# Banded attention: where the reciprocal row sums are transposed, and when the work that closes a head pair is issued

## The chip, the cores and the metric

The kernel runs on one core of one Trainium2 chip. The metric is device time in microseconds (us) of one execution, the median over several runs. A profiled execution also leaves a trace: start, length and releaser of each instruction on each engine.

The engines: PE (TensorE) multiplies matrices and transposes, and writes only to PSUM, a small memory of banks of 128 x 512 floats. DVE (VectorE) and ACT (ScalarE) read PSUM; POOL (GpSimd) works here on the main on-chip memory (SBUF) alone. SP (SyncE) issues all DMAs of this kernel, in order. "PEld" is the load of a matmul's fixed operand; it lies beside the matmul before it.

## The reference, cut to what matters

The model is one inference step of a two-layer encoder. Layer 0 mixes latent attention (A) and a banded attention (B), layer 1 is a windowed attention (C). The change is in B:

```python
B_HEADS, B_HEAD_DIM, CHUNK, B_PAST_CHUNKS, SEQ = 8, 64, 64, 8, 2048

def _grouped_attend(q, k, v, valid, scale, bias=None, sinks=None):
    s = jnp.einsum('...qhgd,...khd->...hgqk', q, k).astype(jnp.float32) * scale
    if bias is not None:
        s = s + bias.astype(jnp.float32)
    s = jnp.where(valid, s, NEG_INF)
    ...
        p = jax.nn.softmax(s, axis=-1)
    return jnp.einsum('...hgqk,...khd->...qhgd', p.astype(v.dtype), v)

# in _ab_layer
    mixed = jnp.concatenate([o_a * jax.nn.silu(g_a), o_b * jax.nn.silu(g_b)], axis=-1)
    return h + _rms(mixed @ w_out, post_g), state
```

Each chunk of 64 queries sees its own chunk and the 8 before it. For the 2048 prompt tokens the kernel works in blocks of 128 queries, each with at most five blocks of 128 keys; 64 sample tokens see 512 cached keys and their own 64.

## The kernel before

The program has five phases: input projections, attention A, attention B together with the output projection of layer 0, input projections of layer 1, attention C with its output projection. Phase 3 is the one that changes. In the trace it lies between about 1323 and 1790 us, with a tail of output projections to about 1842 us.

**Units and steps.** `GROUPS` cuts the 16 query blocks into five groups: blocks 4 to 7, 8 to 11, 12 to 15, then 2 and 3, then 0 and 1. For each group and each of the 8 heads there is one `Unit` for each block: 128 units, and 8 `Sample` units among those of the first group. A loop of 136 calls of `step(n)` runs them as a pipeline. Steps 4 to 135 stand in a `manual_schedule` for PE, DVE, ACT and SP: each of these engines runs its instructions in the order in which the Python code emits them. An engine that waits holds up all that was emitted for it later.

A step emits in this order: the exponentials of unit n+1 (ACT, L1186); the scores of unit n+2 (PE, L1176), their bias and maximum (DVE, L1180); with the first unit of a load, the Q, K and V loads of a later one (SP, L204, L1112, L1147). Then twice: some matmuls of the output projection (`J.pump`, L964) and one `turn`. A `turn` takes one of the two PSUM banks of `ps_t`, lets PE transpose one to three 128 x 128 blocks of probabilities into it (L1203), and ACT copies them to `PT` (L211, the helper `copy`). Its return value, called later in the step as one of the `lows`, lets DVE compute the low part (L214, the helper `lo_of`); with that the bank is free. Between come the products with the values (`av`, PE, L1216) into the single bank of `ps_o`, and, when a head is complete, `out`, which lets ACT copy one half (`tbm`) and DVE add the other into `OT` (L1226).

**Finish.** When both heads of a pair are complete, `out` adds a generator `finish` to the queue `J.side`; there are 24 in all, 20 of the prompt and 4 of the sample. It computes reciprocals of the row sums (DVE, L1237), loads the gate `G` (SP, L1239), spreads the reciprocals over 64 columns a head (ACT, `rb`), transposes this with PE (L1246, one block for each query block) into a bank of `ps_t` of its own, multiplies `OT` by it (DVE, L1247), multiplies by the gate (POOL, L1248) and stores (SP, L1252). `OT` has two buffers and so has the row sum `rsum`: a pair writes the ones that the pair two before it has left. A `yield` ends what one pump of the queue issues; the queue runs its first generator to the end before the next one starts. In the step the pump stands between the first `J.pump` and the first `turn`: one pump, and one more ahead of it if two or more generators are queued (L1414 to L1417).

The last `finish` of a group (`last`) queues the loads of the output projection's token tiles (`token_tile`), which `J.load.pump(1)` at the end of each step drives. After the units, `J.dense` is set and a loop runs the remaining projections.

Of the kernel before, what the change touches and what calls it, by code (L numbers as in the profile page):

```python
# [7 lines left out]
F32 = mybir.dt.float32  # L8
# [8 lines left out]
SEQ, DS, PAST, DM = 2048, 64, 1024, 1024  # L17
# [19 lines left out]
LK, YR3 = 1, 3  # L37
# [73 lines left out]
def kernel(ctx, tc, a, o, upto=5):  # L111

    nc = tc.nc
# [36 lines left out]
    ident = const.tile([128, 128], F32, name="ident")  # L150
# [59 lines left out]
    def copy(out, in_):  # L210
        nc.scalar.activation(out, in_, AF.Copy)  # L211

    def lo_of(out, x, hi, scale=1.0):
        nc.vector.scalar_tensor_tensor(out, x, scale, hi, op0=ALU.mult, op1=ALU.subtract)  # L214
# [822 lines left out]
    def jobs(banks):  # L1037
        J = K()
        J.loaded, J.ready, J.made, J.done, J.banks, J.n, J.credit = False, [], 0, 0, banks, 0, 0.0
        J.last, J.put, J.dense = False, dma, False  # L1040
        J.early, J.half, J.n_early, J.MM = [], {}, 0, {}
        J.side, J.tails, J.load, J.samp = Fill(), Fill(), Fill(), Fill()

        def bank():
            p, n = J.banks[J.n % len(J.banks)]
            J.n += 1
            return p.tile([128, 512], F32, name=n)

        def pump(rate):
            J.credit = min(J.credit + rate, rate + 1)  # L1050
            while J.credit > 0 and next(J.proj):
                J.credit -= 1

        def rest():
            J.load.pump(1)
            (J.side if J.side.q else J.samp).pump(1)
            J.tails.each()
        J.bank, J.pump, J.rest = bank, pump, rest
        return J
# [28 lines left out]
    def phase3():  # L1088
        with ExitStack() as st, ExitStack() as st_a:
# [37 lines left out]
            ps_s, ps_t = pool_a("ps_s3", 2, space=PSUM), pool("ps_t3", 2, space=PSUM)  # L1127
            ps_o, ps_p = pool("ps_o3", 1, space=PSUM), pool("ps_p3", 1, space=PSUM)
            J = jobs([(ps_p, "proj")])
# [4 lines left out]
            for i in range(NPT):  # L1134
                PT = ppt.tile([128, 2, 6, 256], F32R, name=f"PT{i}")
# [5 lines left out]
            def load_values(quad, h0, nh):  # L1141
                start, cnt = GROUPS[quad]
                b0 = max(0, start - 4)
                nb = start + cnt - b0
                V = hv.tile([128, 8, 128], F32R, name="V")[:, :nh * nb].rearrange("p (h b) x -> p h b x", h=nh)
                for h in range(nh):
                    dma(f(V[:, h]), sVB[h0 + h, b0 * 128:(b0 + nb) * 128].rearrange("(b p) x -> p b x", p=128))  # L1147
                    heads[quad, h0 + h].V = V[:, h]

            class Unit:  # L1150
# [42 lines left out]
                def turn(self, g):  # L1193
                    b0, nb = g
                    e = self.i % 2
                    if e == 0 and b0 == 0:
                        self.H.PT = PTs[turn[0] % NPT]
                        turn[0] += 1
                    PT = self.PT = self.H.PT
                    s0 = self.lo - self.base + self.off + b0  # L1200
                    t = ps_t.tile([128, 4, 128], F32, name="t")
                    for b in range(nb):
                        nc.tensor.transpose(t[:, b], self.P[:, (b0 + b) * 128:(b0 + b) * 128 + 128], ident)  # L1203
                    hi = PT[:, 0, s0:s0 + nb, e * 128:e * 128 + 128]
                    copy(hi, t[:, :nb])
                    return lambda: lo_of(PT[:, 1, s0:s0 + nb, e * 128:e * 128 + 128], t[:, :nb], hi)

                def av(self, half):

# [21 lines left out]
            def finish(hp, OT, rs, b0, nb, last=False):  # L1231

                t0 = b0 * 128
                n = min(nb * 128, T - t0)
                b0 = b0 if b0 < 16 else 0
                ri = sc.tile([128, 4, 2], F32, name="ri", bufs=2)
                nc.vector.reciprocal(ri[:, :nb], rs[:, b0:b0 + nb])  # L1237
                G = ot.tile([128, 512], F32, name="G")
                dma(G[:, :n], sG[512 + hp * 128:640 + hp * 128, t0:t0 + n])  # L1239
                rb = sc.tile([128, 4, 2, 64], F32, name="rb", bufs=1)  # L1240
                copy(rb[:, :nb], ri[:, :nb, :, None].to_broadcast([128, nb, 2, 64]))
                for _ in range(YR3 if t0 < 512 or t0 == SEQ else 2):
                    yield
                p = ps_t.tile([128, 512], F32, name="t")
                for b in range(nb):
                    nc.tensor.transpose(p[:, b * 128:b * 128 + 128], rb[:, b].rearrange("p a b -> p (a b)"), ident)  # L1246
                nc.vector.tensor_mul(OT[:, :n], OT[:, :n], p[:, :n])  # L1247
                nc.gpsimd.tensor_tensor(OT[:, :n], OT[:, :n], G[:, :n], op=ALU.mult)  # L1248
                yield
                yield  # L1250
                yield
                dma(sMB[hp * 128:hp * 128 + 128, t0:t0 + n], OT[:, :n])  # L1252
                if last:
                    for d in range(0, n, 128):
                        J.load.add(token_tile(t0 + d, min(128, n - d)))

            def token_tile(t0, r):
                ks = slice(4 if t0 in J.MM else 0, KT)
                M = ld.tile([128, DM], F32, name="M", bufs=1).rearrange("p (k t) -> p k t", k=KT)
                if t0 not in J.MM:  # L1260
                    dma(M[:, 0:4, :r], sM[:, t0:t0 + r].rearrange("(k p) t -> p k t", p=128))
                dma(M[:, 4:8, :r], sMB[:, t0:t0 + r].rearrange("(k p) t -> p k t", p=128))
                for _ in range(2 if J.dense else 4):
                    yield
                while t0 not in J.MM and J.made - J.done >= 2:
                    yield
                J.made += t0 not in J.MM
                MM = J.MM.pop(t0, None) or ld.tile([128, 2, KT, 128], F32R, name="MM", bufs=2)
                copy(MM[:, 0, ks, :r], M[:, ks, :r])
                nc.gpsimd.tensor_tensor(MM[:, 1, ks, :r], M[:, ks, :r], MM[:, 0, ks, :r], op=ALU.subtract)  # L1270
                for _ in range(DRDY3):
                    yield
                J.ready.append((MM, t0, r))
# [95 lines left out]
            def unit(n):  # L1369
                quad, h, j = units[n]  # L1370
                us[n] = Unit(quad, h, j) if j >= 0 else Sample(h)
                us[n].score()
                i = at0.get(units[n], len(loads)) + 1
                if 1 < i < len(loads):
                    load_heads(*loads[i])
                if i < 4:
                    load_bias(i)
                ahead(n + LC)
                keys(n + LK)

            load_values(*loads[0])
            W, us = [], {}
            for n in range(LC):
                ahead(n)
            for n in range(LK):
# [13 lines left out]
            def step(n):  # L1399
                cur = us.pop(n)  # L1400
                if n + 1 in us:
                    us[n + 1].exp()
                if n + 2 < len(units):
                    unit(n + 2)
                quad, h, j = units[n]
                i = at2.get(units[n], len(loads)) + 1
                if 1 < i < len(loads):
                    load_values(*loads[i])
                lows, gs = [], cur.groups()
                rate = RATEA if J.n_early else RATE3 if GROUPS[quad][1] == 4 else RATES  # L1410
                J.samp.pump(1)
                for q in range(2):
                    J.pump(rate / 3)
                    if q == 0:  # L1414
                        if len(J.side.q) > 1:
                            J.side.pump(1)
                        (J.side if J.side.q else J.samp).pump(1)  # L1417
                    if q < len(gs):
                        lows.append(cur.turn(gs[q]))
                if avs:  # L1420
                    v, half = avs.pop(0)
                    v.av(half)
                    if half and v.j == GROUPS[v.quad][1] - 1:
                        late.append(v.out)
                J.pump(rate / 3)
                for fn in lows:
                    fn()
                if cur.j < 0:
                    cur.av(1)
                    late.append(cur.out)  # L1430
                while late:
                    late.pop(0)()
                if cur.j in (1, 3):
                    avs.extend([(cur, 0), (cur, 1)])
                if not J.loaded:
                    J.load.pump(WLOAD)
                J.load.pump(1)
                J.tails.each()

            for n in range(NAUTO3):  # L1440
                step(n)
# [591 lines left out]
```

## Time and profile before

| what | value |
|---|---|
| median of 3 runs | 2735.03 us |
| the 3 runs | 2735.82, 2735.03, 2724.87 us |
| profiled execution, its own time | 2728.87 us |
| its span, first to last instruction | 2727.1 us |
| mean granted TensorE clock | 0.988 |
| DVE, ACT, POOL busy over the span | 1568.7, 1392.4, 522.1 us |

The profiled execution lies 6.2 us below the median and 4.0 us above the fastest run. The four times together have a mean of 2731.15 us. In the views, a wait is the idle time of an engine ahead of an instruction, with the instruction of another engine that ended it; "<-" points to that releaser. In the view of stretches the columns are: the stretch and its length, then busy us and number of instructions of PE, PEld, DVE, ACT and POOL, the granted clock as a share of full speed, the DMA engines' busy share and GB/s.

### The profile page before, as it was taken

What the parts mean: (1) busy time and instruction counts of PE and PEld (TensorE: products, weight loads), DVE (VectorE), ACT (ScalarE), POOL (GpSimd) and SP (SyncE); (2) the same over time, 40 slices, a digit from 0 to 9 for tenths busy, and PEclk for the clock granted to TensorE, in tenths of its full rate; (3) what the DMA queues carried; (4) which work ended last, traced back from release to release, by engine and by line L of the source; (5) the groups of instructions that cost most, each with busy time, mean ns of one, the idle gap of its engine ahead of it and who ended that gap; (6) DMA issues with size and microseconds to landing.
All of it is one profiled execution on the core that took longest, in us unless ns stands there. A gap on an engine that the chain in (4) does not pass through costs nothing. (4 is left out here: it accounts for less than half of the span.)

```text
span 2727.1 us, 46654 instructions
## 1 busy us (share of the span) xinstructions
PE 2566.5 (94%) x16296; PEld 2337.6 (86%) x16296; DVE 1568.7 (58%) x4255; ACT 1392.4 (51%) x3548; POOL 522.1 (19%) x1110
## 2 busy tenths in 40 slices
PE   7999999999999999999888999799999999999997
PEld 6999999899988888888777887679999998787886
DVE  5453345352237778787667766466223214787886
ACT  4332232422337777777666665452233223877783
POOL 0001000001002323211101333342001000344443
PEclk9999999999999999999999999999999998999999
DMA  7546444727447666651666766466425428455552
GB/s 239 171 147 209 133 143 129 255 96 234 143 118 200 194 170 188 167 155 48 194 187 167 204 191 172 149 216 224 149 96 169 127 72 246 109 139 133 137 132 70
DMA packets 382282, 437.92 MB, mean 161 GB/s; under 512 B 49936, under 2 KB 308888, under 8 KB 378816
## 3 DMA queue, kind: packets, MB, share of 16 engines
q1 hardware_dynamic: 382048, 434.95, 54.2%
q8 instruction: 129, 2.11, 0.3%
q14 instruction: 105, 0.86, 0.1%
HBM read 282.80 MB, written 157.09 MB: 161 GB/s over the span
## 5 line engine op out<-in xcount | busy, mean ns | idle before, releaser
L237 PE MATMUL pm<-X,W 128*128 128x384 f32 (+2 forms) x4536 | 752.8, 324 | 2.5 <-DVE ev L214 1.7
L237 PEld LDWEIGHTS pm<-X,W 128*128 128x128 f32 x4536 | 730.4, 189 | 6.2 <-DVE ev L214 2.3
L211 ACT ACTIVATE PT<-t 128x512 fp32r<-128x512 f32 (+3 forms) x704 | 344.5, 504 | 268.9 <-PE t L1203 113.6
L214 DVE SCALAR_TENSOR_TENSOR PT<-t,PT 128x512 fp32r<-128x512 f32 (+3 forms) x688 | 376.0, 569 | 100.8 <-ACT PT L211 99.3
L964 PE MATMUL proj<-Wo,MM 128*128 128x512 f32 (+1 forms) x1416 | 391.6, 407 | 11.3 <-ACT z L211 8.1
L964 PEld LDWEIGHTS proj<-Wo,MM 128*128 128x128 f32 (+1 forms) x1416 | 246.1, 187 | 59.5 <-ACT z L211 11.6
L214 DVE SCALAR_TENSOR_TENSOR ev<-pm,ev 128x256 fp32r<-128x256 f32 (+3 forms) x197 | 98.6, 502 | 336.9 <-ACT ev L430 102.2
L237 PE MATMUL pm<-W,X 128*128 128x256 f32 (+5 forms) x2040 | 281.2, 297 | 0.0
L237 PEld LDWEIGHTS pm<-W,X 128*128 128x128 f32 (+1 forms) x2040 | 272.0, 187 | 1.0
L702 ACT ACTIVATE P<-s,m 128x512 f32<-128x512 f32 (+9 forms) x344 | 209.3, 616 | 33.3 <-DVE m L691 30.7
L683 PE MATMUL s<-KA,Q 128*128 128x512 f32 (+7 forms) x640 | 201.1, 396 | 10.5 <-ACT P L702 8.4
L228 DVE TENSOR_TENSOR W<-R,W 128x768 fp32r<-128x768 f32 (+3 forms) x114 | 116.0, 1055 | 134.0 <-ACT W L227 133.7
L726 PE MATMUL t<-ident,P 128*128 128x128 f32 x1088 | 176.3, 276 | 3.4 <-ACT P L702 1.0
L689 DVE TENSOR_REDUCE m<-s 128x1 f32<-128x480 f32 (+7 forms) x216 | 132.4, 613 | 80.3 <-PE s L683 79.9
L726 PEld LDWEIGHTS t<-ident,P 128*128 128x128 f32 x1088 | 134.6, 141 | 41.7 <-ACT P L702 15.1
L754 PE MATMUL acc<-PT,V 128*128 128x256 f32 x1152 | 156.3, 285 | 6.6 <-DVE OT L763 6.6
L754 PEld LDWEIGHTS acc<-PT,V 128*128 128x128 f32 x1152 | 140.6, 188 | 12.0 <-PE t L726 6.0
L1702 ACT ACTIVATE P<-s,m 128x256 f32<-128x256 f32 (+2 forms) x264 | 119.4, 465 | 11.6 <-DVE m L1694 10.3
L1216 PE MATMUL acc<-PT,V 128*128 128x256 f32 x672 | 111.6, 298 | 13.7 <-DVE OT L1226 11.0
L1180 DVE CUSTOM_DVE_ANT_0 s<-s,bias 128x640 f32<-128x640 f32 (+4 forms) x128 | 95.4, 745 | 42.9 <-PE s L1176 40.7
L1693 DVE CUSTOM_DVE_ANT_0 s<-s,mask 128x256 f32<-128x256 f32 (+1 forms) x256 | 107.6, 422 | 20.2 <-PE t L1711 10.9
L683 PE MATMUL s<-KR,Q 128*128 128x384 f32 (+6 forms) x320 | 116.2, 363 | 0.6 <-DMA Q<-sQR 0.6
(248 smaller groups left out, 3927.7 us busy)
## 6 DMA issues: line engine op xcount, KB each, us to landing
Q<-sQA SPq DMA_DIRECT2D x128, 128.0 KB, 3.3
sWO<-W SPq DMA_DIRECT2D x32, 512.0 KB, 3.8
Q<-sQB SPq DMA_DIRECT2D x128, 128.0 KB, 3.1
Wo<-sWO SPq DMA_DIRECT2D x16, 1024.0 KB, 8.8
Q<-sQC SPq DMA_DIRECT2D x32, 512.0 KB, 7.7
R<-in_ab_w_in_dram SPq DMA_DIRECT2D x40, 384.0 KB, 4.1
K<-sKB SPq DMA_DIRECT2D x56, 256.0 KB, 5.6
V<-sVB SPq DMA_DIRECT2D x24, 512.0 KB, 6.7
```

Of the source, the lines that this page charges most:

```text
L211: nc.scalar.activation(out, in_, AF.Copy)
L214: nc.vector.scalar_tensor_tensor(out, x, scale, hi, op0=ALU.mult, op1=ALU.subtract)
L228: nc.vector.tensor_tensor(Wv[:, 1, k0:k1], Rv, Wv[:, 0, k0:k1], op=ALU.subtract)
L237: nc.tensor.matmul(ps, lhs(x, k), rhs(y, k), start=(j == 0), stop=(j == n - 1))
L683: nc.tensor.matmul(s[:r, :n], self.Q[:, x, self.qo:self.qo + r], rhs, start=(x == 0), stop=(x == 2))
L689: nc.vector.tensor_reduce(m[:r, j:j + 1], s[:r, :n], axis=AX.X, op=ALU.max)
L702: nc.scalar.activation(self.P[:r, o0:o0 + n], self.s.pop(j)[:r, :n], AF.Exp, bias=self.m[:r, 6:7], accum_out=acc)
L726: nc.tensor.transpose(t[:, b], self.P[:, (b0 + b) * 128:(b0 + b + 1) * 128], ident)
L754: nc.tensor.matmul(acc[:, (i // 2) % 2], H.V[:, b0 + b], PT[:, x, b], start=(b0 + b == 0 and x == 0), stop=(b0 + b == i and x == 1))
L964: nc.tensor.matmul(p, M[:, x, k, :r], W[k][:, y, cs], start=(k == k0 and t == 0), stop=(k == k1 - 1 and t == 2))
L1216: nc.tensor.matmul(acc, self.H.V[:, self.base - self.H.b0 + b], self.PT[:, x, off + b], start=(b == 0 and x == 0), stop=(b == nblk - 1 and ...
L1702: nc.scalar.activation(self.P[:, c, :w], self.s[:, c, :w], AF.Exp, bias=m[:, 1, c:c + 1], accum_out=m[:, 0, c:c + 1])
```

## The change

`finish` no longer takes a bank. It puts its transposes, one for each query block, into a list `spreads`. Each `turn` (none has more than three blocks of its own) takes one of them and transposes it into the last quarter of its own bank; after the low part DVE multiplies that 128 columns of `OT`. The reciprocal and the ACT copy that reads it now come in different pumps. What is still listed when the units have ended is transposed in a bank as before. In `step` the pump of `J.side` moves from between the first projection matmuls and the first `turn` to the end of the step: `J.rest()` holds one pump each of `J.load` and of `J.side` (or, if this is empty, `J.samp`) and a round of `J.tails`; with two or more generators queued, two pumps come ahead of it. Between the gate's multiplication and the store lie two yields, not three.

```diff
                     for b in range(nb):
                         nc.tensor.transpose(t[:, b], self.P[:, (b0 + b) * 128:(b0 + b) * 128 + 128], ident)
+
+                    while spreads and not spreads[0]:
+                        spreads.pop(0)
+                    out = None
+                    if spreads and nb < 4:
+                        x, out = spreads[0].pop(0)
+                        nc.tensor.transpose(t[:, 3], x, ident)
                     hi = PT[:, 0, s0:s0 + nb, e * 128:e * 128 + 128]
                     copy(hi, t[:, :nb])
-                    return lambda: lo_of(PT[:, 1, s0:s0 + nb, e * 128:e * 128 + 128], t[:, :nb], hi)
+
+                    def low():
+                        lo_of(PT[:, 1, s0:s0 + nb, e * 128:e * 128 + 128], t[:, :nb], hi)
+                        if out is not None:
+                            nc.vector.tensor_mul(out, out, t[:, 3, :out.shape[-1]])
+                    return low
...
                 dma(G[:, :n], sG[512 + hp * 128:640 + hp * 128, t0:t0 + n])
+                yield
                 rb = sc.tile([128, 4, 2, 64], F32, name="rb", bufs=1)
                 copy(rb[:, :nb], ri[:, :nb, :, None].to_broadcast([128, nb, 2, 64]))
-                for _ in range(YR3 if t0 < 512 or t0 == SEQ else 2):
+                yield
+                todo = [(rb[:, b].rearrange("p a b -> p (a b)"), OT[:, b * 128:min(n, b * 128 + 128)]) for b in range(nb)]
+                spreads.append(todo)
+                while todo and not J.dense:
                     yield
-                p = ps_t.tile([128, 512], F32, name="t")
-                for b in range(nb):
-                    nc.tensor.transpose(p[:, b * 128:b * 128 + 128], rb[:, b].rearrange("p a b -> p (a b)"), ident)
-                nc.vector.tensor_mul(OT[:, :n], OT[:, :n], p[:, :n])
+                if todo:
+                    p = ps_t.tile([128, 4, 128], F32, name="t")
+                    for b, (x, _) in enumerate(todo):
+                        nc.tensor.transpose(p[:, b], x, ident)
+                    for b, (_, y) in enumerate(todo):
+                        nc.vector.tensor_mul(y, y, p[:, b, :y.shape[-1]])
+                    todo.clear()
                 nc.gpsimd.tensor_tensor(OT[:, :n], OT[:, :n], G[:, :n], op=ALU.mult)
-                yield
                 yield
                 yield
                 dma(sMB[hp * 128:hp * 128 + 128, t0:t0 + n], OT[:, :n])
...
-            W, us = [], {}
+            W, us, spreads = [], {}, []
...
                     J.pump(rate / 3)
-                    if q == 0:
-                        if len(J.side.q) > 1:
-                            J.side.pump(1)
-                        (J.side if J.side.q else J.samp).pump(1)
                     if q < len(gs):
                         lows.append(cur.turn(gs[q]))
...
-                J.load.pump(1)
-                J.tails.each()
+                if len(J.side.q) > 1:
+                    J.side.pump(2)
+                J.rest()
```

## Prediction

> **What bounds the kernel now.** I read the page's busy times, the view of stretches over phase 3, PE's waits there, and the timeline around each wait.
>
> ```profile
> PE 2566.5 (94%) x16296; PEld 2337.6 (86%) x16296; DVE 1568.7 (58%) x4255; ACT 1392.4 (51%) x3548; POOL 522.1 (19%) x1110
> 1345.00:1456.00 111.00, 94.74 (x653) 76.77 (x652) 70.43 (x190) 68.66 (x178) 7.28 (x12) 0.98 0.70 196
> 1456.00:1550.00 94.00, 85.44 (x576) 74.84 (x576) 71.13 (x183) 63.06 (x152) 23.08 (x45) 1.00 0.75 197
> 1700.00:1790.00 90.00, 71.52 (x359) 57.56 (x358) 38.66 (x137) 42.01 (x122) 38.89 (x74) 0.94 0.51 155
> ```
>
> PE is busy 94% of the span. Its work doesn't change (68 transposes of `rb` before and after), so the change is worth what it takes from PE's idle time in phase 3: 16.3 and 8.6 us in the stretches of the first two groups, 18.5 us in that of the two short groups. No other engine is near its limit there; DVE comes nearest, with 71 of 94 us. PE's waits in the stretch from 1345 to 1778 us (total us, times, longest):
>
> ```profile
> PE proj L964 <- ACT z L211: 8.1, 6, 2.3
> PE t L1203 <- DVE OT L1247: 7.5, 11, 1.5
> PE t L1203 <- DVE PT L214: 7.4, 10, 1.8
> PE t L1246 <- DVE PT L214: 3.8, 3, 1.8
> PE t L1203 <- DVE OTs L1247: 2.3, 4, 0.8
> PE t L1300 <- DVE PT L214: 2.0, 2, 1.3
> ```
>
> They come in clusters, each around one `finish`. The timeline of one:
>
> ```profile
> 1508.34 0.19 DVE L1237 RECIPROCAL ri<-rsum 128x8 f32<-128x8 f32 x1
> 1508.57 0.63 ACT L211 ACTIVATE rb<-ri 128x512 f32<-128x512 f32 x1 [1.72 <-DVE ri L1237]
> 1510.22 0.77 PE L1203 MATMUL t<-ident,P 128*128 128x128 f32 x5 [1.79 <-DVE PT L214]
> 1513.21 0.66 PE L1246 MATMUL t<-ident,rb 128*128 128x128 f32 x4 [0.74 <-DVE PT L214]
> 1515.70 0.44 PE L1203 MATMUL t<-ident,P 128*128 128x128 f32 x2 [1.51 <-DVE OT L1247]
> ```
>
> The reciprocal stands behind the scores' work in DVE's queue; ACT waits 1.72 us for it, and the copy of `t` that should free a bank stands behind ACT: PE waits 1.79 us. Two steps later the finish's own bank enters the rotation: PE waits 0.74 us for it, then 1.51 us for the wide multiplication to give it back.
>
> **What goes.** *The copy behind its reciprocal.* Seven of the ten waits on L214 ahead of L1203 and both on L1300 end within 1.7 us of the start of an `rb` copy, like the one above; the three others are 0.8 us together, so 7.4 - 0.8 = 6.6, and 2.0. All three on L1246 go with their instruction: 3.8. One on the projection belongs here:
>
> ```profile
> 1645.83 0.63 ACT L211 ACTIVATE rb<-ri 128x512 f32<-128x512 f32 x1 [1.72 <-DVE ri L1237]
> 1647.37 0.96 PE L964 MATMUL proj<-Wo,MM 128*128 128x512 f32 x3 [2.27 <-ACT z L211]
> ```
>
> Sum 6.6 + 2.0 + 3.8 + 2.3 = 14.7 us. After the change the copy is emitted a whole step behind its reciprocal.
>
> *The bank of its own*: the waits on L1247, 7.5 + 2.3 = 9.8 us.
>
> *Row sums given back late.* In the short groups a pair has only four units. I followed the generators through the loop by hand, with steps counted from 0: the reciprocals of five pairs are issued in steps 115, 119, 123, 127 and 131, each just the step whose exponential writes the same buffer of `rsum`:
>
> ```profile
> 1723.19 0.37 ACT L1186 ACTIVATE P<-s,m 128x128 f32<-128x128 f32 x1 [1.98 <-DVE ri L1237]
> 1724.19 1.67 PE L964 MATMUL proj<-Wo,MM 128*128 128x512 f32 x6 [1.67 <-ACT z L211]
> 1753.28 0.37 ACT L1186 ACTIVATE P<-s,m 128x128 f32<-128x128 f32 x1 [2.13 <-DVE ri L1237]
> 1756.52 0.79 PE L1216 MATMUL acc<-PT,V 128*128 128x256 f32 x2 [2.15 <-DVE rs L187]
> 1766.49 0.37 ACT L1186 ACTIVATE P<-s,m 128x128 f32<-128x128 f32 x1 [2.44 <-DVE ri L1237]
> 1767.49 1.66 PE L964 MATMUL proj<-Wo,MM 128*128 128x512 f32 x6 [1.68 <-ACT z L211]
> ```
>
> After the change they are issued at the ends of steps 113, 117, 121, 125 and 129. This gives 1.67 + 2.15 + 1.68 = 5.5 us.
>
> *OT stored late.* The store of a pair and the first write of the pair two later lie in the same step, again only in the short groups:
>
> ```profile
> 1711.63 1.22 PE L1216 MATMUL acc<-PT,V 128*128 128x256 f32 x4 [3.43 <-DVE OT L1226]
> 1743.87 0.42 DVE L1226 TENSOR_TENSOR OT<-acc,tbm 64x256 f32<-64x256 f32 x1 [3.61 <-DMA sMB<-OT]
> 1744.34 0.50 PE L1216 MATMUL acc<-PT,V 128*128 128x256 f32 x2 [1.59 <-DVE OT L1226]
> ```
>
> The first wait is for the store of the third group's last pair, which moves only from step 110 (behind that step's loads) to the end of 109: I take 2.5 of its 3.43. The stores of the five pairs behind it move from steps 115 to 131 to about two steps earlier: 1.59 in full. Sum 4.1 us.
>
> Together **34.1 us** of PE's idle time has its cause removed.
>
> **What comes.** DVE's wide multiplications become narrow ones:
>
> ```profile
> L1247 DVE TENSOR_TENSOR OT<-OT,t 128x512 f32<-128x512 f32 x12 | 8.2, 681 | 0.5 <-PE t L1246 0.3
> L1247 DVE TENSOR_TENSOR OT<-OT,t 128x256 f32<-128x256 f32 x6 | 2.5, 417 | 4.9 <-PE t L1246 4.9
> L1247 DVE TENSOR_TENSOR OTs<-OTs,t x4: 203/210/211, 1369.6 to 1453.1; 128x64 f32<-128x64 f32 x4
> 1503.20 0.49 PE L1203 MATMUL t<-ident,P 128*128 128x128 f32 x3
> 1504.22 0.38 PE L1203 MATMUL t<-ident,P 128*128 128x128 f32 x2
> ```
>
> A width of 128 isn't in the trace; between 210 ns (64) and 417 ns (256) it is 0.28 us by a straight line. 64 x 0.28 replaces 12 x 0.68 + 8 x 0.41: DVE gains 6.4 us of work in all, beside PE. What can reach PE is the bank: with a guest in it, ACT's copy starts one transpose later (0.49 - 0.38 = 0.11 us) and DVE frees it 0.28 us later: 0.39 us for each of the 64 guests (20 in the first group, 16, 16, 8 and 4 in the others; the last four transposes come after the loop). Between finishes a bank has room:
>
> ```profile
> 1505.06 0.42 DVE L214 SCALAR_TENSOR_TENSOR PT<-t,PT 128x256 fp32r<-128x256 f32 x1 [0.25 <-ACT PT L211]
> 1506.43 0.71 PE L1203 MATMUL t<-ident,P 128*128 128x128 f32 x5
> 1434.92 0.63 ACT L211 ACTIVATE rb<-ri 128x512 f32<-128x512 f32 x1 [1.07 <-DVE ri L1237]
> 1436.58 0.77 PE L1203 MATMUL t<-ident,P 128*128 128x128 f32 x5 [1.81 <-DVE PT L214]
> L211 ACT ACTIVATE rb<-ri x24: 308/522/631, 1356.2 to 1782.3; 128x512 f32<-128x512 f32 x12, 128x256 f32<-128x256 f32 x8, 128x128 f32<-128x128 f32 x4
> ```
>
> In the second group both banks are free at 1505.48, and PE comes 0.95 us later: 0.39 disappears in that. In the first group fewer projection matmuls lie between, and ACT's delay of 1.07 + 0.63 came out as 1.81 us on PE: no room. There I expect part of the guests (20 x 0.39 = 7.8) and of the `rb` copies' own time, which stays (four of 0.63 and four sample copies of 0.31, the shortest in the row: 3.8 us): bounds 0 and 11.6, I take 7.0, nearer to the upper end because the row at 1436.58 has no room. For the other 44 guests the bounds are 0 and 17.2; I take 2.5, by the row at 1506.43.
>
> The Trainium skill, "VectorE: DVE Perf Modes", section "Rules for kernel authors", speaks against this part: minimize the number of DVE operations, since the flush behind each is paid whatever the chaining. The rows agree that narrow ones are dear (64 columns cost 210 ns, eight times as many 681), and by that rule the bill is the upper end of both bounds, which is the second rival below.
>
> POOL's and ACT's work stays as it is. SP: in four finishes (steps 109, 125, 129, 133) two generators are queued, so gate multiplication and store fall into one pump and SP waits for POOL, with the next step's Q, K and V loads and the projection's loads behind it. Such waits stand in the trace now and PE shows one late load:
>
> ```profile
> SPq L1252 <- POOL OTs L1248: 17.7, 3, 9.2
> PE s L1176 <- DMA K<-sKB: 2.9, 1, 2.9
> ```
>
> I cost this at 0, as loads go out four units ahead; without that cover it is 4 x 2.9 = 11.6 us.
>
> *Clock.* Two stretches of 10 us in the short groups:
>
> ```profile
> 1710.00:1720.00 10.00, 8.37 (x39) 7.09 (x40) 5.72 (x16) 2.60 (x7) 0.74 (x2) 0.83 0.70 209
> 1750.00:1760.00 10.00, 7.64 (x34) 6.22 (x33) 3.54 (x19) 4.97 (x15) 7.30 (x16) 0.83 0.75 239
> ```
>
> Each loses 10 x 0.17 = 1.7 us of clock, some 1.4 us of PE's work, and each holds a wait named above (3.43 and 2.15 us). Bounds 0 and 2.8; I take 1.4, as the first isn't sure to go whole. The Trainium skill, "TensorE: Matmul & The Clock Gate", section "Why this matters for your kernels", warns of gaps over about 3 us alone; by that only the first would count, while the second row shows a low clock with none longer than 2.15 us.
>
> **Sum**: -34.1 + 7.0 + 2.5 - 1.4 = **-26.0 us**. The profiled execution took 2728.87 us (span 2727.1 and 1.8 around it), 6.2 below the median of the three runs. I set the sum against the mean of all four times, 2731.2: **2705 us**. What is late next in these steps is PE's own chain: the single bank of `ps_o` behind `tbm`, ACT's `z` copies, and PE's work itself.
>
> **The rivals.** *Every guest is paid* (0.20): all bounds at their upper end, 17.2 + 11.6 = 28.8 against 34.1 + 1.4: -6.7, 2724.5 us. For it: DVE has 71 of 94 us in the second group. Against it: all but 0.8 of the 7.4 us of waits on L214 lie in steps of a finish, so the others have room.
>
> *The waits only move* (0.10): the 14.7 + 9.8 us come back as waits on `z`, `tbm` or scores, since ACT has the same copies to make; only 5.5 + 4.1 stays: -9.6, 2721.6 us. For it: 8.1 us on `z` now. Against it: most of those lie behind an `rb` or its reciprocal.
>
> *Slower* (0.08): the round from PE over ACT and DVE back to PE sets the pace of a step, not the bank. Then nothing of the 24.5 us is won, and each guest lengthens the round: at 0.39 us 25.0, at 0.417 + 0.11 us (a narrow multiplication as dear as one of 256 columns) 33.7, less 9.6: +15.4 to +24.1, about 2747 to 2755 us. It decides once the room at 1506.43 is below 0.39 us in all groups, not only in the first. Against it: that room is 0.95 us.
>
> **How the numbers follow.** The forecast (0.62) reaches from -36.9 (nothing paid, the clock in full) to where a measurement begins to tell it: 2694 to 2717.5. The first two rivals lie at 2722 and 2725; with the runs' own spread of some 5 us either way the range is 2690 to 2730, which leaves out the last rival and the ends. About 0.5% (13.7 us) is what a measurement of this kernel tells from no change: faster 0.62, the two rivals inside it 0.30, slower 0.08.
>
> **What would show it.** In the changed trace: no PE wait on a multiplication L1247 carried; ACT's idle time ahead of `rb` near 0; exponentials without a wait on the reciprocal; no DVE wait on sMB<-OT; PE's busy time in phase 3 unchanged in a stretch some 25 us shorter; narrow multiplications of about 280 ns. The forecast is wrong if waits on L214 grow beyond 10 us, if PE waits on K or Q, or if what is won before 1790 us is lost in phase 4, whose order a scheduler sets anew.

## The result and the profile after

| | before | after |
|---|---|---|
| median | 2731.09 us (4 runs) | 2688.33 us (4 runs) |
| range | 2724.87 to 2735.82 | 2687.56 to 2696.46 |
| profiled execution, span | 2727.1 us | 2685.8 us |

Three runs, one each of the kernel before, of e1 and of the changed kernel, took 12100, 6273 and 3940 us and are left out of all figures below. The ratio is 0.9848, with a 95% interval of 0.9820 to 0.9876: faster by some 41 us, of which the interval allows 34 to 49. The forecast was faster by 26 us, 2705 us, with a range of 2690 to 2730. The direction was right, the size was too small, and the time lies 1.7 us below the range.

The view of stretches, cut at the same units in both traces: from the ninth unit's scores to the 41st (the first group with its sample units), to the 73rd, to the 105th, and to the last (the two short groups). First the kernel before:

```profile
1350.58:1450.18 99.60, 84.10 (x576) 67.67 (x577) 62.07 (x167) 60.80 (x158) 6.96 (x11) 0.98 0.67 182
1450.18:1548.58 98.40, 89.13 (x606) 78.26 (x606) 74.50 (x192) 66.22 (x160) 22.48 (x41) 1.00 0.76 197
1548.58:1660.27 111.69, 105.51 (x679) 92.75 (x679) 76.20 (x191) 70.36 (x165) 34.84 (x66) 1.00 0.68 184
1660.27:1773.69 113.42, 97.47 (x507) 79.50 (x506) 55.95 (x190) 57.96 (x169) 39.84 (x86) 0.95 0.57 160
```

and the changed one:

```profile
1355.16:1441.10 85.94, 81.87 (x576) 66.37 (x575) 62.19 (x175) 59.99 (x157) 6.88 (x11) 1.00 0.71 193
1441.10:1533.69 92.59, 89.39 (x610) 79.40 (x610) 74.64 (x204) 66.12 (x159) 24.38 (x53) 1.00 0.82 210
1533.69:1637.95 104.26, 102.27 (x668) 91.13 (x666) 75.98 (x203) 69.99 (x166) 31.82 (x55) 1.00 0.73 197
1637.95:1741.19 103.24, 95.68 (x515) 78.11 (x514) 56.44 (x199) 58.32 (x169) 40.78 (x87) 0.98 0.65 177
```

Length less PE's busy time is PE's idle time: 15.5, 9.3, 6.2 and 16.0 us before, 4.1, 3.2, 2.0 and 7.6 us after, so 46.9 and 16.8 in all. PE's busy time falls too, from 376.2 to 369.2 us, with the same work (2368 and 2369 matmuls in the rows); the clock column (last but two) rises in the first and the last row. The gain of 37.1 us in these stretches is therefore 30.1 us of idle time and 7.0 us of PE running faster.

PE's waits in the changed trace, 1345 to 1778 us (total, times, longest); line numbers have moved, L1210 is the guest's transpose, L1217 its multiplication, L1228 the product with the values, L1238 the sum into `OT`:

```profile
PE acc L1228 <- DVE OT L1238: 4.5, 4, 2.2
PE proj L964 <- ACT z L211: 3.1, 8, 0.7
PE t L1203 <- DVE OT L1217: 2.9, 6, 1.0
PE acc L1228 <- DVE rs L187: 2.0, 1, 2.0
PE t L1203 <- DVE PT L214: 1.7, 4, 0.7
PE t L1210 <- ACT rb L211: 1.2, 3, 0.6
PE s L1176 <- DMA K<-sKB: 0.6, 1, 0.6
```

The wide multiplication's 9.8 us are gone; 2.9 us stand at its narrow successors. The waits on L214 fell from 7.4 to 1.7 us. The finish that the prediction showed at 1508 us, in the timeline of the changed kernel:

```profile
1494.90 0.20 DVE L1249 RECIPROCAL ri<-rsum 128x8 f32<-128x8 f32 x1
1497.12 0.63 ACT L211 ACTIVATE rb<-ri 128x512 f32<-128x512 f32 x1
1497.61 0.77 PE L1203 MATMUL t<-ident,P 128*128 128x128 f32 x5 [0.73 <-DVE PT L214]
1501.21 0.27 PE L1210 MATMUL t<-ident,rb 128*128 128x128 f32 x1
1502.02 0.38 PE L1203 MATMUL t<-ident,P 128*128 128x128 f32 x2
1502.52 0.28 DVE L1217 TENSOR_TENSOR OT<-OT,t 128x128 f32<-128x128 f32 x1
```

ACT's copy no longer waits here; over the phase its wait ahead of `rb` is 3.2 us, where it was 19.0. PE loses 0.73 us where it lost 1.79 + 0.74 + 1.51. The narrow multiplications, by the view of their line (shortest, median and longest in ns, then first and last start in us):

```profile
L1217 DVE TENSOR_TENSOR OT<-OT,t x60: 276/277/280, 1376.5 to 1743.0; 128x128 f32<-128x128 f32 x60
```

277 ns is the 0.28 us that the prediction read off a straight line.

### The profile page after: what moved, and what is told of

The parts are those of the page before. It is cut to its first block, busy times and chain, and to the rows that moved or that the text cites. A ratio compares the mean times of both kernels' runs of the same rounds, so it can differ in the third digit from the quotient of the medians.

```text
span 2685.8 us, 46771 instructions
## 1 busy us (share of the span) xinstructions
PE 2562.0 (95%) x16296; PEld 2337.2 (87%) x16296; DVE 1568.8 (58%) x4299; ACT 1391.8 (52%) x3548; POOL 520.5 (19%) x1110
## 4 chain that ended last, share of the span: by engine, by line
PE 79%; DVE 9%; ACT 5%; DMA 3%; issue 3%; POOL 1%; SPq 0%; ACTq 0%; DVEq 0%; POOLq 0%
PE pm L237 39%; PE proj L964 10%; PE s L683 6%; PE acc L754 4%; PE t L726 3%; PE acc L1228 3%; DVE PT L214 2%; PE s L1176 2%; PE t L1203 2%; PE t L1726 2%; PE acc L1733 2%; PE s L1705 1%; ACT P L702 1%; DVE m L689 1%; DVE s L1708 1%
## 5 line engine op out<-in xcount | busy, mean ns | idle before, releaser
L214 DVE SCALAR_TENSOR_TENSOR PT<-t,PT 128x512 fp32r<-128x512 f32 (+3 forms) x688 | 377.2, 569 | 91.6 <-ACT PT L211 89.0
L214 DVE SCALAR_TENSOR_TENSOR ev<-pm,ev 128x256 fp32r<-128x256 f32 (+3 forms) x197 | 98.6, 503 | 336.0 <-ACT ev L430 101.2
L1228 PE MATMUL acc<-PT,V 128*128 128x256 f32 x672 | 111.5, 298 | 6.7 <-DVE OT L1238 4.5
L1180 DVE CUSTOM_DVE_ANT_0 s<-s,bias 128x640 f32<-128x640 f32 (+4 forms) x128 | 95.2, 744 | 35.1 <-PE s L1176 33.5
```

The lines of the kernel that those rows point to most:

```text
L1228: nc.tensor.matmul(acc, self.H.V[:, self.base - self.H.b0 + b], self.PT[:, x, off + b], start=(b == 0 and x == 0), stop=(b == nblk - 1 and ...
```

## The experiments

Three edits make up the change: **split** (the copy one pump behind its reciprocal), **late** (the pump at the end of the step) and **guests** (transposes in the turns' banks; the yield that is gone ahead of the store goes with them). The experiments run each alone, each pair, and the guests' cost doubled. The table has the results; e8 and e9 repeat the two kernels, and e11 gave none (see e2). A ratio is against the runs of the kernel before that were taken with that kernel. "Idle" is PE's idle time in the four stretches above, cut at the same units in each kernel's own trace. "Same clock" is from a fit to the 75 runs whose clock is on record: one constant for each kernel and one slope against the run's granted clock, which came out as -2.0 us for 0.001; the column gives the constant at 0.988, less that of before (2726.4). Its uncertainty is some 3 us, and it leaves out what an edit does to the clock itself. The runs come from several chips; at the same clock the kernel before agrees between them within about 1 us. In the idle column one wait goes by chance: PE's wait for a late load of K is 2.9 us in the first trace of before and 1.0 in the second, 0.6 and none in the changed kernel's two, and up to 3.6 in the others.

| kernel | median, us | ratio to before, interval | idle, us | same clock, us |
|---|---|---|---|---|
| before | 2731.09 | | 46.9 (second trace 44.3) | 0 |
| e1: split | 2722.01 | 0.9964 (0.9946 to 0.9982) | 40.5 | -9.6 |
| e2: late | 2707.19 | 0.9915 (0.9889 to 0.9941) | 28.2 | -21.3 |
| e3: guests | 2712.81 | 0.9934 (0.9905 to 0.9963) | 34.2 | -18.9 |
| e5: split, late | 2697.04 | 0.9876 (0.9856 to 0.9896) | 26.2 | -28.2 |
| e6: split, guests | 2706.75 | 0.9909 (0.9884 to 0.9934) | 28.7 | -23.6 |
| e7: guests, late | 2701.07 | 0.9886 (0.9858 to 0.9915) | 22.7 | -23.5 |
| all three | 2688.33 | 0.9848 (0.9820 to 0.9876) | 16.8 (17.1) | -35.1 |
| e4: all, guests' transpose and product twice | 2701.50 | 0.9896 (0.9862 to 0.9931) | 23.0 | -22.9 |
| e10: all, guests' product twice | 2699.02 | 0.9881 (0.9857 to 0.9906) | 24.0 | -25.6 |

### e1: the split alone

```diff
                 dma(G[:, :n], sG[512 + hp * 128:640 + hp * 128, t0:t0 + n])
+                yield
                 rb = sc.tile([128, 4, 2, 64], F32, name="rb", bufs=1)
                 copy(rb[:, :nb], ri[:, :nb, :, None].to_broadcast([128, nb, 2, 64]))
-                for _ in range(YR3 if t0 < 512 or t0 == SEQ else 2):
+                for _ in range((YR3 if t0 < 512 or t0 == SEQ else 2) - 1):
                     yield
```

> The kernel before with one edit: the ACT copy rb one pump behind its reciprocal, the number of pumps up to the transposes kept. Theory S (the sources add up: copy behind its reciprocal 14.7 us, bank of its own 9.8, row sums and stores in the short groups 9.6): the 14.7 us go, about 2716 us, ACT's idle time ahead of rb near 0, waits on the own bank still there. Rival P (the place of the pump is what counts; the others mostly repeat it): at most 4 us, 2727 to 2731 us.

Some 10 us went, not 14.7, and not the 4 us at most of rival P. Idle time fell by 6.4 us or, against the second trace of before, 3.8. ACT's wait ahead of `rb` did go, mostly. ACT's idle time ahead of this copy in e1, by the view of the tile `rb`:

```profile
its engine sat idle before it (us, times) until:
  DVE ri L1237: 4.1, 5
```

PE's waits in e1, 1345 us to the last unit, did not follow it:

```profile
PE t L1203 <- DVE OT L1248: 7.9, 11, 2.2
PE t L1203 <- DVE PT L214: 3.8, 6, 1.2
PE t L1247 <- DVE PT L214: 3.5, 3, 1.8
```

ACT's 19 us became 4.1, yet only 3.6 of the 7.4 us on L214 went and almost nothing of the 3.8 us at the own bank's transposes (here L1247).

### e2: the late pump alone

```diff
                 for q in range(2):
                     J.pump(rate / 3)
-                    if q == 0:
-                        if len(J.side.q) > 1:
-                            J.side.pump(1)
-                        (J.side if J.side.q else J.samp).pump(1)
...
-                J.load.pump(1)
-                J.tails.each()
+                if len(J.side.q) > 1:
+                    J.side.pump(2)
+                J.rest()
```

> The kernel before with one edit: the pump of J.side at the end of the step (two pumps more with two or more queued), reciprocal and copy still in one pump, own bank kept. Theory S: row sums and stores come earlier, 9.6 us go, about 2721 us. Rival P: 20 us or more go, 2711 us or less, as the copy no longer stands ahead of a turn's copies.

Some 24 us, as rival P had it, and the larger share of the whole change. PE's longest waits in e2, 1345 to 1778 us:

```profile
PE proj L964 <- ACT z L211: 9.4, 8, 2.8
PE t L1246 <- DVE PT L214: 8.3, 9, 1.8
PE s L1176 <- ACT P L1186: 5.7, 7, 1.7
PE t L1203 <- DVE PT L214: 1.3, 2, 0.7
```

ACT's waits in e2, one line, 1345 to 1768 us:

```profile
ACT rb L211 <- DVE ri L1237: 17.4, 20, 2.4
```

ACT still waits 17.4 us for reciprocals, nearly as before. The waits ahead of L1216 fell from 11.8 us (9.6 on L1226, 2.2 on L187) to 0.9: these are the row sums and stores of theory S. What theory S didn't have: the bank of its own is still there, and the 9.8 us that PE waited for it to come back, which the prediction had given to the guests, are gone from the list. The timeline shows why. First the kernel before, at the finish that the prediction showed:

```profile
1513.98 0.82 DVE L1180 CUSTOM_DVE_ANT_0 s<-s,bias 128x640 f32<-128x640 f32 x1
1514.97 0.68 DVE L1247 TENSOR_TENSOR OT<-OT,t 128x512 f32<-128x512 f32 x1
```

and a finish in e2:

```profile
1480.20 0.66 PE L1246 MATMUL t<-ident,rb 128*128 128x128 f32 x4 [0.54 <-DVE PT L214]
1480.61 0.84 PE L1176 MATMUL s<-K,Q 128*128 128x320 f32 x4
1480.89 0.69 DVE L1247 TENSOR_TENSOR OT<-OT,t 128x512 f32<-128x512 f32 x1 [0.42 <-PE t L1246]
1481.28 0.79 PE L1203 MATMUL t<-ident,P 128*128 128x128 f32 x5
```

Inside the step the scores' work (L1180) stands ahead of the wide multiplication in DVE's queue: the multiplication starts 1.76 us after the transposes at 1513.21, and the `turn` comes right behind them. At the step's end the multiplication starts 0.69 us after the transposes, PE has the next step's scores to compute meanwhile, and the `turn` at 1481.28 doesn't wait.

What is left moved to the finish's own instructions and to what is queued behind the waiting copy. PE's waits on L214 fell from 7.4 to 1.3 us ahead of the turns but rose from 3.8 to 8.3 ahead of L1246; those on `z` rose from 8.1 to 9.4, those on exponentials from 0.9 to 5.7. In the second and third full group two generators are queued in one step alone (step 41, by following the loop), so the extra pumps play next to no part there: their idle time fell from 9.3 and 6.2 to 5.1 and 3.0 us by the place.

A pump right behind the two turns of the same step would test the place by itself; e11 was written for that and gave no time, because its order deadlocks. By the code, the finish's transposes ask for a third bank while the two turns hold both, and DVE has the finish's multiplication ahead of the low parts that would free one. So the extra pumps and the place aren't separated in the first group and in the short ones.

### e3: the guests alone

```diff
                 ri = sc.tile([128, 4, 2], F32, name="ri", bufs=2)
                 nc.vector.reciprocal(ri[:, :nb], rs[:, b0:b0 + nb])
...
-                yield
                 rb = sc.tile([128, 4, 2, 64], F32, name="rb", bufs=1)
...
                     J.pump(rate / 3)
+                    if q == 0:
+                        if len(J.side.q) > 1:
+                            J.side.pump(1)
+                        (J.side if J.side.q else J.samp).pump(1)
...
-                if len(J.side.q) > 1:
-                    J.side.pump(2)
-                J.rest()
+                J.load.pump(1)
+                J.tails.each()
```

(against the changed kernel.)

> The changed kernel with the pump put back into the step and the reciprocal and its copy in one pump: only the transposes as guests are left of the change. Theory S: the waits on the own bank go (9.8 us, and 0.7 of those ahead of it), about 2720 us, ACT still waits some 19 us ahead of rb. Rival G (guests are paid, 0.39 us each in the first group): 2726 us or more. Rival P: 2727 to 2731 us.

Some 18 us, more than theory S gave and against both rivals. PE's waits in e3:

```profile
PE t L1210 <- ACT rb L211: 12.7, 8, 3.1
PE t L1203 <- DVE PT L214: 8.1, 8, 1.8
```

ACT's idle time ahead of `rb` in e3, by the view of that tile:

```profile
its engine sat idle before it (us, times) until:
  DVE ri L1249: 19.0, 21
```

The wide multiplication's waits are gone, the copy's 19 us are all there. A new wait of 12.7 us appears: with two generators queued, copy and guests can fall into the same step, and PE waits for ACT. All eight of these waits lie in the first and the short groups, where two are queued. In the changed kernel this is 1.2 us.

### e4 and e10: the guests' cost doubled

```diff
                         nc.tensor.transpose(t[:, 3], x, ident)
+                        nc.tensor.transpose(t[:, 3], x, ident)
...
+                            gx = sc.tile([128, 128], F32, name="gx", bufs=1)
+                            nc.vector.tensor_mul(gx[:, :out.shape[-1]], out, t[:, 3, :out.shape[-1]])
                             nc.vector.tensor_mul(out, out, t[:, 3, :out.shape[-1]])
```

(e10 has only the second part.)

> The changed kernel with each guest's transpose and its multiplication by DVE done twice (the second product goes to a scratch tile nobody reads): 64 more transposes and 64 more narrow multiplications. The prediction's cost of guests (0.39 us each where a bank has no room, 9.5 us in all) doubled: 2688 + 9 or more, 2697 us or later, with more waits of PE on the guests' multiplication in the first group. Rival (a guest costs next to nothing, a few us of PE's own time): 2688 to 2693 us.

> The changed kernel with only DVE's narrow multiplication of each guest done twice (the second product goes to a scratch tile nobody reads); the transposes once. With both twice it was 12 us slower at the same clock, of which 64 transposes of 0.11 us on PE make 7. Theory: what is left, some 5 us, is the multiplication in the bank's way: 2693 to 2698 us. Rival (DVE's part is hidden, the transposes with their later copies make it all): 2688 to 2692 us.

Both are slower than the changed kernel, by 12 and 9.5 us at the same clock. e4 came in as its theory had it; e10 lies 1 us above its own, within the noise. The transposes, for which e10's text set 7 us, come out at the 2.7 us between the two, which is within the 3 us of uncertainty. e10's trace says where:

```profile
PE t L1203 <- DVE OT L1219: 6.5, 14, 0.8
PE t L1210 <- ACT rb L211: 2.0, 3, 1.4
```

A second narrow multiplication behind each guest raises PE's wait on this line (here L1219) from 2.9 us in 6 waits to 6.5 in 14, and idle time by 7.2 us, of which 1.6 are the wait for K. So a guest is not free, and the theory's direction was right. But 58 of the 64 guests of the changed kernel make PE wait for no multiplication: all 64 cost the 2.9 + 1.2 = 4.1 us that its trace shows, where the prediction set 9.5. By the same two lines the second ones add 4.4 us, so they aren't shown to be dearer than the first.

### e5, e6, e7: the pairs

> Own bank kept; copy one pump behind its reciprocal and pump at the end of the step. By the medians alone split gave 10 us, the late pump 25, guests 20, the whole change 43. Theory A (the parts add up): about 2698 us. Theory O (the split and the late pump take away the same wait, an rb copy ahead of a turn's copy): no better than the late pump alone, 2704 to 2710 us, with PE's waits on the own bank as in the kernel before.

> Pump inside the step as before; split and guests. Theory A: 30 us, about 2703 us. Theory O says the same here, as these two take away different waits. What stays by both: exponentials that wait for a reciprocal and OT waiting for its store in the short groups, some 10 us.

> The changed kernel with reciprocal and copy in one pump again, at the end of the step. Theory A: 45 us less the split's share, about 2698 us by the whole change of 43 and 10 of the split. Theory O: the split adds nothing behind the late pump, 2686 to 2693 us.

Split and late together gave 28.2 us at the same clock, close to 9.6 + 21.3: theory A, and theory O falls. In idle time the split adds less behind the late pump, 2.0 us (4.4 without the waits for K). Guests and late overlap: 23.5, far less than 18.9 + 21.3. e7 lies 3 us from theory A's time and well above theory O's: without the split some 10 us are missing. Split and guests gave 23.6 of 28.5, against the 30 us of both theories. In the four stretches they do add up (18.2 us of idle time, of 6.4 + 12.7); the rest lies behind these, where the tail and phase 4 take 498.1 us in e6, 494.0 in e1 and 493.9 in e3. Read from the whole change, the last edit to be added gives 6.9 us (guests), 11.6 (split) or 11.5 (late). PE's longest waits in e5, without guests:

```profile
PE t L1247 <- DVE PT L214: 9.0, 11, 1.8
PE proj L964 <- ACT z L211: 7.3, 8, 1.8
```

And in e7, without the split:

```profile
PE s L1176 <- ACT P L1186: 7.6, 12, 1.0
PE proj L964 <- ACT z L211: 7.5, 7, 2.8
```

Behind a late pump, the guests take away the wait to get a bank (9.0 us), not that to give it back. The split, there, takes away waits on exponentials and `z` (0.7 and 3.1 us in the changed trace); that these stand behind a waiting `rb` copy is read from the order of the code.

### e8, e9: both kernels once more

> The changed kernel once more, unchanged, for a second trace. Theory L (a share of the 43 us is the granted clock's luck in the executions compared): at a clock of 0.988 it takes some 2688 us and the kernel before some 2725, so 37 us apart; phase 5, whose code is the same, differs between traces of one kernel by as much as the 5 us seen between the kernels. Rival: phases 4 and 5 are shorter by 3 and 5 us again.

> The kernel before once more, for a second trace. Theory L (luck of the granted clock): PE's idle time from the ninth to the last unit of phase 3 is 47 us again, within 2; phase 5 takes 451 to 460 us, as in the other traces, and so isn't shorter by 5 us because of the change; the tail and phase 4 take 496 or 497 us again if their order sets that, 490 to 494 if not. Rival: phase 5 takes 457 us again within 0.5.

The changed kernel took 2689.69 us, the median of three runs (ratio 0.9856, 0.9830 to 0.9883), before 2726.68 us in one run. Idle time in the four stretches is 17.1 and 44.3 us; the second lies 0.7 us outside what theory L allowed, and the wait for K is 1.9 us shorter in that trace. So the difference belongs to the kernels. The stretches from the last unit to the end of phase 4 and from there to the end, by the view of stretches, before:

```profile
1773.69:2270.30 496.61, 486.62 (x3075) 473.19 (x3074) 181.38 (x499) 151.82 (x305) 55.72 (x73) 1.00 0.49 155
2270.30:2727.10 456.80, 418.02 (x2340) 349.39 (x2338) 351.67 (x953) 316.78 (x944) 179.47 (x381) 0.97 0.51 133
```

before again:

```profile
1776.38:2272.80 496.42, 486.57 (x3075) 473.23 (x3074) 181.55 (x499) 151.94 (x305) 55.90 (x73) 1.00 0.49 155
2272.80:2724.90 452.10, 414.16 (x2340) 344.54 (x2338) 350.88 (x952) 316.43 (x944) 179.43 (x381) 0.98 0.51 134
```

after:

```profile
1741.19:2234.50 493.31, 486.89 (x3074) 474.25 (x3073) 181.46 (x501) 151.25 (x305) 54.22 (x73) 0.99 0.49 157
2234.50:2685.80 451.30, 412.44 (x2340) 343.79 (x2338) 351.03 (x952) 316.87 (x944) 179.68 (x381) 0.98 0.51 134
```

after again:

```profile
1740.06:2233.90 493.84, 487.28 (x3073) 474.30 (x3072) 180.67 (x501) 151.36 (x305) 54.25 (x73) 0.99 0.49 156
2233.90:2687.90 454.00, 414.79 (x2340) 345.90 (x2338) 351.20 (x952) 316.80 (x944) 179.65 (x381) 0.98 0.51 134
```

The tail and phase 4 are shorter by 3.3 us in the first pair and 2.6 in the second, while two traces of one kernel agree within 0.5: that is the change's doing, and PE's idle time there falls by 3.4 us (10.0 and 9.9 to 6.4 and 6.6). Phase 5 takes 456.80 and 452.10 us in the same kernel: the 5.5 us between the first pair of traces are mostly luck, as theory L said, and the rival of a phase 5 that is shorter by 5 us again falls: in the second pair it is 1.9 us longer.

## Why the forecast had the direction and missed the size

Taking the mean of two traces each, the span fell by 39.2 us: 28.6 us of PE's idle time in the four stretches (45.6 to 17.0), 7.7 us of PE's busy time there (376.9 to 369.2), 2.9 us in the tail and phase 4, 1.8 us in phase 5, less 1.9 us for all that lies ahead of the ninth unit. Against the steps of the prediction:

- **PE is the bound, and its idle time in phase 3 is what can be won: right.** Its instructions stayed the same, DVE and ACT stayed off the bound.
- **34.1 us of waits lose their cause: right as a sum, with one term wrong.** 46.9 us of idle time became 16.8. The exponentials' waits on reciprocals and DVE's waits on stores of `OT` are gone from the lists of the changed trace, and PE waits 0.6 us for K, so SP's cost of 0 held. But the 2.15 us on L187, put down to a late reciprocal, did not go: both traces of the changed kernel have this wait with 2.0 us, though no exponential waits for a reciprocal there. PE waits there for the bank of `ps_o`, whose copy `tbm` stands behind a `z` copy on ACT. That the sum held all the same is in part luck: the waits on L1226 gave 5.1 us (9.6 to 4.5) where 4.1 was set.
- **What belongs to which edit: wrong.** The prediction gave 14.7 us to the split, 9.8 to the guests and 9.6 to the earlier row sums and stores, and nothing to the place of the pump in the long groups. Alone, the split cut idle time by 6.4 us, the late pump by 18.7, the guests by 12.7. The place alone removed the whole wait for the own bank's return, and the waits on L214 ahead of the turns; of those ahead of the own bank it made more. Ending ACT's wait, by the split, took only about half of the waits on L214 ahead of the turns (7.4 to 3.8 us).
- **"What comes", 7.0 + 2.5 = 9.5 us: too dear, the first failed term.** It assumed that an `rb` copy's own 0.63 us still stands ahead of a turn and that the first group has no room for a guest. In the changed kernel the copy stands at the end of the step, and the room was there: 4.1 us of waits at guests remain, and the first group's idle time fell from 15.5 to 4.1 us.
- **Clock, -1.4 us with a bound of 2.8: too small, the second failed term and the larger miss.** The rows of the four stretches lose 7.7 us of clock before (each length times what the clock falls short of 1) and 2.1 after; PE's busy time fell by 7.0 us (7.7 by the mean of two traces each). Over the runs with a clock on record its mean is 0.9858 before (29 runs) and 0.9884 after (7 runs), which at 2.0 us for 0.001 is 5 us. The prediction counted two stretches of 10 us and left out the first group, where the clock was 0.98.
- **The tail and phase 4: left out.** 2.9 us, of which the sum had nothing; the prediction named phase 4 only as a place where a gain might be lost. In other kernels this stretch moves more: with the late pump alone it takes 489.6 us, 6.9 less than before, and with split and guests 498.1.

These 39.2 us are 13.2 more than the forecast's 26.0: idle time fell by 4.0 us more than the 34.1 - 9.5 = 24.6 forecast, since the cost was too dear, PE's busy time by 6.3 more than the clock's 1.4, and the tail and phase 4 give 2.9. The mean of the runs (2730.8 to 2690.4) tells the same, 14 us beyond. None of the rivals came in. The first (every guest is paid) has a true core, as e10 shows, but most guests found room. The second (the waits only move) shows in single edits: e2's waits on `z` and exponentials. The slower one needed that room to vanish in all groups, which the 58 guests without such a wait contradict.

Why the clock is higher after isn't shown by an experiment. Idle time alone doesn't order it: the mean clock of the runs is 0.987 to 0.990 in the six kernels with the late pump and 0.985 to 0.986 in the four without, though e2 and e6 have nearly the same idle time (28.2 and 28.7 us). Why the tail and phase 4 are 2.9 us shorter is open too.

## What to carry to other kernels

On an engine that runs in the order of the code, ask of a waiting instruction what stands right ahead of it and right behind it: moving the whole group to where other work lies behind it gave 21 us, of which some 7 lie in the tail and phase 4; ending ACT's wait where it stood gave 10. When several edits aim at one stall, sum the stalls, not the edits, and give each edit to the trace alone before saying which one pays. A guest in a bank cost little here because the banks had room: 6 of 64 made PE wait for their multiplication, 14 when it was done twice.

## What the runs showed of the hardware

The granted clock moves the time of one and the same kernel: in e1's runs 0.981 took 2733.21 us and 0.988 took 2716.76. A gap of the same length at the same place can go with a clock drop or not. At the start of phase 3 PE waits 1.76 us in the trace of before and 1.75 us in that of after; the view of stretches, before:

```profile
1323.00:1345.00 22.00, 18.01 (x127) 14.57 (x127) 12.42 (x31) 9.97 (x25) 6.37 (x19) 1.00 0.77 272
```

and after:

```profile
1323.00:1345.00 22.00, 18.67 (x107) 15.28 (x108) 10.39 (x26) 7.78 (x20) 6.15 (x18) 0.74 0.79 276
```

The clock is 1.00 in one and 0.74 in the other, and the changed kernel is 4.6 us behind at its ninth unit. That is not the change's doing: in the second traces the same gap is 1.76 us in both kernels, the clock in this stretch 0.78 before and 0.70 after, and the changed kernel 0.7 us ahead at its ninth unit. The Trainium skill, "TensorE: Matmul & The Clock Gate", Part 1, says that the window over which the clock gate watches PE runs freely, so that the moment of a transition varies from run to run; these rows agree with it, though gaps of 1.75 us are shorter than the 3 us that its section "Why this matters for your kernels" warns of.
